# Shift rows as VectorE sums and late corrections in the first part of a hybrid-attention layer

## Chip, cores and metric

The kernel runs on one core of one Trainium2 chip. The metric is the device time of one execution in microseconds (us). The kernel before takes 2448.01 us, the median of three runs (2447.83 to 2448.09).

## The reference, cut to what matters

One transformer layer of width 2048 works on 512 latent tokens and 256 context tokens, in float32:

```python
mod_x = silu(c) @ w_ada + b_ada            # 6 x 2048 values for the latents
mod_c = silu(c_ctx) @ w_ada + b_ada        # the same for the context
h  = rmsnorm(x, norm1_w)   * (1 + s1)  + sh1     # shift sh1 and scale s1 from mod_x
hc = rmsnorm(ctx, norm1_w) * (1 + s1c) + sh1c    # from mod_c
p  = h @ w_in ;  pc = hc @ w_in            # queries, keys, values of 8 + 8 heads
x  = x + g1 * (attention heads of p, pc) @ w_o
x  = x + g2 * conv_ffn(modulate(rmsnorm(x, norm2_w), sh2, s2))
```

The change concerns sh1, s1 and the product with w_in. That product is linear: shifting the tokens by sh1 adds the vector sh1 @ w_in to every row of p.

## The kernel before

Tokens stand transposed: 16 tiles (kt) of 128 model channels, each with 512 latent columns and 256 context columns. Every float32 operand of a large product is cut into a rounded high half and the rest (ScalarE casts the high half, VectorE subtracts; `split`, lines L80 and L81), and `mm3` multiplies high by high, high by low and low by high (L104 to L106). Weight blocks are loaded raw (wr) and split into wh and wl, three buffers each. In the rows below a2k and c2k are token tiles, kh and kl split results on their way to DRAM, s and b accumulators in PSUM.

The stages up to the first head are:

- **First features.** The squares of the tokens are summed for the norm. Then for each unit of two kt the modulation is made: `scales` multiplies four 512 KB loads (adak) with silu(c) on TensorE (16 products, L219) and turns the result with `sel` (L223); `shifts` makes sh1 for both kt. For even kt it is four row sums of 1024 on VectorE (L251). For odd kt it is 16 transposes on TensorE (L258), four ScalarE copies (wt, L259) and 16 products (L219 with wt). Tokens get norm, scale and shift (L330 to L333) and go through `mm3` against five blocks of w_in: the four accumulators for latents and context, and one for the first query.
- **Features.** Seven blocks of 128 features (`feature`), each with rope, split and a write to DRAM (`keys`); then three blocks for the compressed query (`cq`) without context.
- **Values.** `for half in range(2)`: eight weight blocks each, 288 products, six accumulators; then each accumulator is split through two kvs buffers and written to v_d, from SP's queue for half 0 and from POOL's for half 1.
- **First head.** Its keys (ks, L527) are read back from DRAM; the score products are L482.

64 later values of the modulation are gemvs: `gemv` loads a row block of 1 MB (ada) over SP's queue into one of two buffers, and VectorE sums it (L171). 48 of them are handed out by `next_gemv` between the blocks of the features and values: 3 per feature, 2 per cq block, 1 or 2 per block of values. The order on each engine is set by a scheduler that follows the program's order where data and buffers allow; from the MLP on it is written by hand.

## Time and profile before

| | us |
|---|---|
| median of three runs | 2448.01 |
| profiled execution | 2454.1 |
| its span | 2451.9 |
| TensorE matmuls busy in the span | 2375.5 |
| VectorE busy | 1726.3 |
| ScalarE busy | 1102.5 |

The profiled execution is one run under the profiler, 2.2 us longer than its span; the mean granted TensorE clock was 0.988. The stretches named in the prediction are us from the span's start. Engines: PE is TensorE, DVE VectorE, ACT ScalarE, POOL GpSimd, SP SyncE, which issues most transfers. "L171" is line 171 of the kernel. In the lists of groups stand line, engine, operation, output and inputs, shapes and count, then busy time, mean ns of one, and idle time before it with what ended it.

### The profile page before, as it was taken

What the parts mean: (1) busy time and instruction counts of PE and PEld (TensorE: products, weight loads), DVE (VectorE), ACT (ScalarE), POOL (GpSimd) and SP (SyncE); (2) the same over time, 40 slices, a digit from 0 to 9 for tenths busy, and PEclk for the clock granted to TensorE, in tenths of its full rate; (3) what the DMA queues carried; (4) which work ended last, traced back from release to release, by engine and by line L of the source; (5) the groups of instructions that cost most, each with busy time, mean ns of one, the idle gap of its engine ahead of it and who ended that gap; (6) DMA issues with size and microseconds to landing.
All of it is one profiled execution on the core that took longest, in us unless ns stands there. A gap on an engine that the chain in (4) does not pass through costs nothing.

```text
span 2451.9 us, 32940 instructions
## 1 busy us (share of the span) xinstructions
PE 2375.5 (97%) x12788; PEld 1988.9 (81%) x12788; DVE 1726.3 (70%) x2272; ACT 1102.5 (45%) x1666; POOL 242.1 (10%) x270
## 2 busy tenths in 40 slices
PE   7999999999999999999999999999999999999997
PEld 3778887877777778888888888888888888888887
DVE  4668785388868877377666666666666666666667
ACT  4342121155545542244545454545454545454553
POOL 0000000122100003100111111111111111111113
PEclk8999999999999999999999999999999999999999
DMA  7868898554411149423555655555555555555572
GB/s 276 283 228 297 321 340 289 189 181 137 141 59 44 44 159 337 152 85 112 134 141 135 141 135 141 134 142 134 140 135 143 133 143 133 144 132 142 133 213 78
DMA packets 130706, 403.31 MB, mean 164 GB/s; under 512 B 14323, under 2 KB 25075, under 8 KB 122099
## 3 DMA queue, kind: packets, MB, share of 16 engines
q1 hardware_dynamic: 104118, 350.87, 43.4%
q0 software_dynamic: 25280, 49.30, 11.5%
q8 instruction: 100, 1.64, 0.3%
q10 hardware_dynamic: 1152, 1.05, 0.1%
q14 instruction: 56, 0.46, 0.1%
HBM read 331.68 MB, written 69.48 MB: 164 GB/s over the span
## 4 chain that ended last, share of the span: by engine, by line
PE 84%; DVE 8%; ACT 3%; DMA 3%; issue 1%; POOL 1%; SPq 0%; DVEq 0%; ACTq 0%; POOLq 0%
PE y L973 12%; PE b L105 10%; PE b L104 10%; PE b L106 10%; PE z L973 6%; PE y L975 6%; PE z L975 3%; PE s L104 3%; PE s L105 3%; PE s L106 3%; PE s L482 3%; PE x L973 2%; DMA ada<-in_ada 2%; PE x L975 1%; PE f L104 1%
## 5 line engine op out<-in xcount | busy, mean ns | idle before, releaser
L104 PE MATMUL b<-ah,wh 128*128 128x512 f32 (+1 forms) x672 | 259.1, 386 | 0.0
L105 PE MATMUL b<-al,wh 128*128 128x512 f32 (+1 forms) x672 | 259.0, 385 | 0.0
L106 PE MATMUL b<-ah,wl 128*128 128x512 f32 (+1 forms) x672 | 258.0, 384 | 0.0
L994 POOL DMA_DIRECT2D x_d<-xs x160 | 139.7, 1003 | 1166.4 <-ACT xs L993 1164.3
L949 DVE TENSOR_TENSOR wl<-wr,wh 128x1024 fp32r<-128x1024 f32 x126 | 153.8, 1221 | 128.7 <-ACT wh L943 128.7
L949 DVE TENSOR_TENSOR wl<-rb,wh 128x1024 fp32r<-128x1024 f32 x124 | 151.2, 1220 | 128.0 <-ACT wh L943 128.0
L80 ACT CAST wh<-wr 128x1024 fp32r<-128x1024 f32 (+3 forms) x118 | 115.9, 982 | 259.0 <-PE b L105 68.3
L943 ACT CAST wh<-wr 128x1024 fp32r<-128x1024 f32 x126 | 132.3, 1050 | 206.3 <-PE b L105 100.7
L943 ACT CAST wh<-rb 128x1024 fp32r<-128x1024 f32 x124 | 130.2, 1051 | 190.0 <-PE b L105 112.5
L949 DVE TENSOR_TENSOR wl<-ws,wh 128x1024 fp32r<-128x1024 f32 x123 | 150.1, 1221 | 88.8 <-ACT wh L943 88.8
L81 DVE TENSOR_TENSOR wl<-wr,wh 128x1024 fp32r<-128x1024 f32 (+3 forms) x118 | 137.3, 1164 | 89.4 <-ACT wh L80 89.0
L171 DVE CUSTOM_DVE_ANT_0 ada<-ada,cb,smt 128x2048 f32<-128x2048 f32 x64 | 151.6, 2369 | 62.4 <-DMA ada<-in_ada 62.1
L943 ACT CAST wh<-ws 128x1024 fp32r<-128x1024 f32 x123 | 128.3, 1043 | 137.0 <-PE b L105 45.2
L106 PEld LDWEIGHTS b<-ah,wl 128*128 128x128 f32 x672 | 126.3, 188 | 25.6
L104 PEld LDWEIGHTS b<-ah,wh 128*128 128x128 f32 x672 | 126.6, 188 | 22.9
L105 PEld LDWEIGHTS b<-al,wh 128*128 128x128 f32 x672 | 126.6, 188 | 22.0
L104 PE MATMUL b<-a2k,wh 128*128 128x512 f32 (+1 forms) x352 | 133.1, 380 | 6.6 <-ACT a2k L756 5.0
L106 PE MATMUL b<-a2k,wl 128*128 128x512 f32 (+1 forms) x352 | 132.5, 376 | 0.0
L973 PE MATMUL y<-b2k,wh 128*128 128x512 f32 x410 | 106.9, 390 | 0.0
L484 DVE TENSOR_REDUCE m<-s 128x1 f32<-128x768 f32 x96 | 90.5, 949 | 15.3 <-PE s L482 14.9
L993 ACT ACTIVATE xs<-b,modx 128x512 f32<-128x512 f32 x160 | 101.0, 680 | 0.5 <-PE y L973 0.3
L973 PEld LDWEIGHTS y<-b2k,wh 128*128 128x128 f32 x410 | 77.0, 188 | 17.1
(471 smaller groups left out, 5937.4 us busy)
## 6 DMA issues: line engine op xcount, KB each, us to landing
ada<-in_ada SPq DMA_DIRECT2D x64, 1024.0 KB, 6.8
rb<-in_w_up SPq DMA_DIRECT2D x123, 512.0 KB, 4.4
wr<-in_w_dn SPq DMA_DIRECT2D x84, 512.0 KB, 4.3
x_d<-xs POOLq DMA_DIRECT2D x160, 256.0 KB, 6.0
wr<-in_w_up SPq DMA_DIRECT2D x53, 512.0 KB, 4.2
wr<-in_w_f SPq DMA_DIRECT2D x34, 512.0 KB, 5.9
adak<-in_ada_k SPq DMA_DIRECT2D x32, 512.0 KB, 6.2
ada<-in_ada SPq DMA_DIRECT2D x32, 512.0 KB, 6.6
```

Of the source, the lines that this page charges most:

```text
L80: sc.copy(dst_h, src)
L81: ve.tensor_tensor(dst_l, src, dst_h.bitcast(F32), op=ALU.subtract)
L104: pe.matmul(out, st[0], mv[0], start=start, stop=False, **kw)
L105: pe.matmul(out, st[0], mv[1], start=False, stop=False, **kw)
L106: pe.matmul(out, st[1], mv[0], start=False, stop=stop, **kw)
L171: ve.tensor_tensor_reduce(out=junk, in0=w, in1=vec, op0=ALU.mult, op1=ALU.add, scale=1.0, scalar=col("b_ada", j), accum_out=dst[:, j:j + 1])
L943: sc.copy(hi, raw)
L949: ve.tensor_tensor(lo, raw, hi.bitcast(F32), op=ALU.subtract)
L973: pe.matmul(o, w[j][0], hs[j], start=start and j == 0, stop=False, skip_group_check=True)
L975: pe.matmul(o[:, h0], w[j][1], hs[j][:, h0], start=False, stop=j == 7, skip_group_check=True)
L993: sc.mul(x, po, modx[:, 80 + dt:81 + dt])
L994: gp.dma_start(x1_d[dt], x, accum_op=ALU.add)
```

## The change

The whole stretch from the start to the end of the first half of the values is written out in one order for all five engines; the code behind it is left to the scheduler.

- Scale products run one unit ahead, from eight loads of 256 KB per unit. Squares use the weight buffers.
- `shifts` is gone: no transposes, wt copies or wt products. A shift is now two row sums of 2048 on VectorE (`row_sum`), its 1 MB row loaded over POOL's queue (`row_load`).
- In the first features only kt 8 to 15 are shifted; kt 0 to 7 go in unshifted. The five results, and the sixth from an early feature that follows, are kept raw. During the early feature and the first half of the values VectorE sums the rows of kt 0 to 7, and `add_shift` adds them to the tokens, which are split again. The first half of the values takes the blocks in the order 4 to 7, 0 to 3.
- `bias_products` makes what the unshifted tokens lack in the six raw results, sh1 times w_in, in four steps, one behind each half of the next two features; it loads these weights again over POOL's queue, into the two ada buffers. `with_bias` adds it on ScalarE. The keys, first query and latent norm made from raw results move behind the second and third of these features.
- All gemv loads go over POOL's queue. Counts: 1 for each of the last three blocks of the first half of values, 2, 2, 2 and then 3 per feature, 3 per cq block and 3 per block of the second half. The second half's value writes stay on POOL.

```diff
-    def gemv(pool, j, srcs, bufs=2):
+    def gemv(pool, j, srcs, bufs=2, queue=None):
...
-        nc.sync.dma_start(w, ada[j])
+        (queue or nc.sync).dma_start(w, ada[j])
...
-        wt = st.tile([P, KT, P], F32, tag="wt", name=nm("wt"), bufs=1)
-        for q in range(4):
-            for i in range(4):
-                k = (q % 2) * 4 + i
-                pe.transpose(acc[:, i * P:(i + 1) * P], ws[q // 2][:, k * P:(k + 1) * P], ident)
-            sc.copy(wt[:, 4 * q:4 * q + 4].rearrange("p k f -> p (k f)"), acc)
-        products(lambda kt: wt[:, kt], P)
-        for i, d in enumerate(dst):
-            ve.tensor_scalar(out=d, in0=acc[:, i:i + 1], scalar1=col("b_ada", kt), scalar2=None, op0=ALU.add)
...
+    KA, EARLY = 8, 1
+    KB = ((4, 5, 6, 7, 0, 1, 2, 3), tuple(range(8)))
...
+    def row_load(kt):
+        rows[kt] = sp_.tile([P, D], F32, tag="ada", name=nm("ada"), bufs=2)
+        gp.dma_start(rows[kt], ada[kt])
+
+    def row_sum(kt, i):
+        w = rows[kt]
+        vec, m = ((cb, modx), (ccb, modc))[i]
+        out = w if i else sp_.tile([P, D], BF16, tag="junk", name=nm("junk"), bufs=1)
+        ve.tensor_tensor_reduce(out=out, in0=w, in1=vec, op0=ALU.mult, op1=ALU.add, scale=1.0,
+                                scalar=col("b_ada", kt), accum_out=m[:, kt:kt + 1])
+
+    def add_shift(kt, tmp):
+
+        for i, (hl, m, n_) in enumerate(((hx[kt], modx, T), (hc[kt], modc, C))):
+            t = tmp()[:, :n_]
+            ve.tensor_tensor(t, hl[0].bitcast(F32), hl[1].bitcast(F32), op=ALU.add)
+            split_hl(hl, t, m[:, kt:kt + 1])
...
+        def scale_load(u):
+            wks[u] = []
...
+            for j in range(8):
+                wk = st.tile([P, 2, 2 * P], F32, tag="adak", name=nm("adak"), bufs=9)
+                nc.sync.dma_start(wk, ada_k[u, j // 4][:, (j % 4) * 2:(j % 4) * 2 + 2])
+                wks[u].append(wk)
...
+        def tokens_b(kt):
+            h = hs.pop(kt)
+            for hl, c, m in ((hx[kt], slice(0, T), modx), (hc[kt], slice(T, TT), modc)):
+                split_hl(hl, h[:, c], m[:, kt:kt + 1] if kt >= KA else None)
...
+        due = [(kt, i) for kt in range(KA, KT) for i in range(2)][1:]
+        NU = KT // 2
+        for u in range(NU):
+            if u + 2 < NU:
+                scale_load(u + 2)
+            raws_ = [wraw(w_g0[kt], 640) for kt in (2 * u + 2, 2 * u + 3)] if u + 1 < NU else []
+            if u + 2 < NU:
+                row = scale_products(u + 2)
+            if u + 1 < NU:
+                for kt in (2 * u + 2, 2 * u + 3):
+                    tokens_a(kt)
+                for kt, raw in zip((2 * u + 2, 2 * u + 3), raws_):
+                    if kt >= KA:
+                        while due and due[0][0] <= kt:
+                            row_sum(*due.pop(0))
+                    tokens_b(kt)
+                    block_g0(raw)
+            else:
+                ahead(2)
+            first_features(2 * u)
+            if u + 2 < NU:
+                scale_turn(u + 2, row)
+            for _ in range(2 if u else 3):
+                if due:
+                    kt, i = due.pop(0)
+                    row_sum(kt, i)
+                    if i and kt + 2 < KT:
+                        row_load(kt + 2)
+            first_features(2 * u + 1)
...
-                gemv(pool, j, [(cb, modx)])
-
-    lo, hi = slice(0, 64), slice(64, 128)
+                gemv(pool, j, [(cb, modx)], queue=gp)
...
-    latent_norm(ckv, TT, KVR, "kvn", ckv_d)
-    for f in range(7):
-        lat, co = b_tile(), s_tile()
-        feature(lat, co[:, :C])
-        keys(k_d[f + 2] if f < 6 else kr_d, lat, co[:, :C])
-        next_gemv(kv, 3)
-    cq = []
-    for i in range(3):
-        lat = b_tile()
-        feature(lat, None)
-        t = kv.tile([P, TT], F32, tag="lt", name=nm("cq"), bufs=3)[:, :T]
-        sc.copy(t, lat)
-        cq.append(t)
-        next_gemv(kv, 2)
...
-            next_gemv(kv, 1 if (half * 8 + kb) % 3 else 2)
...
+        raws[4] = keep(lat0[4], None, rawq)
+        for f in (2, 3, 0, 1):
+            raws[f] = keep(lat0[f], ctx0[f])
+        todo = [(kt, i) for kt in range(KA) for i in range(2)]
+
+        def sums_of_rows(count):
+            for _ in range(count):
+                if todo:
+                    kt, i = todo.pop(0)
+                    row_sum(kt, i)
+                    if i and kt + 2 < KA:
+                        row_load(kt + 2)
+
+        def early(hf):
+            sums_of_rows(2)
+            ahead(2)
+
+        elat, eco = b_tile(), s_tile()
+        feature(elat, eco[:, :C], early)
+        raws[5] = keep(elat, eco[:, :C])
+
+        def upper(n_):
+            ahead(2)
+            if n_ < 4:
+                sums_of_rows(3)
+                for kt in ((0, 1), (2,), (3,), (4, 5))[n_]:
+                    add_shift(kt, rtmp)
+            elif n_ == 4:
+                for kt in (6, 7):
+                    add_shift(kt, rtmp)
+            else:
+                next_gemv(sp_, 1)
+
+        vo0 = values(0, upper)
...
+        w = sp_.tile([P, D], F32, tag="ada", name=nm("bw"), bufs=2)
+        if step < 3:
+            kts = range(3 * step, min(3 * step + 3, KA))
+            for i, kt in enumerate(kts):
+                gp.dma_start(w[:, i * 640:(i + 1) * 640], w_g0[kt])
+            for i, kt in enumerate(kts):
+                r = slice(32 * (kt % 4), 32 * (kt % 4) + 32)
+                o = i * 640
+                pe.matmul(ac[0][r], spad[:, kt], w[:, o:o + 512], start=kt < 4, stop=kt >= KA - 4)
+                pe.matmul(ac[1][r, :P], spad[:, kt], w[:, o + 512:o + 640], start=kt < 4, stop=kt >= KA - 4,
+                          skip_group_check=True)
+            return
+        gp.dma_start(w[:, :1024], w_f[0, 0])
+        for kt in range(KA):
+            r = slice(32 * (kt % 4), 32 * (kt % 4) + 32)
+            pe.matmul(ac[1][r, P:2 * P], spad[:, kt], w[:, kt * P:(kt + 1) * P], start=False, stop=kt >= KA - 4,
+                      skip_group_check=True)
+        for n_, c in enumerate((4, 2)):
+            row = rtmp()
+            sc.copy(row[:, :c * P], ac[n_][:, :c * P])
+            for i in range(c):
+                pe.matmul(ac[n_][:, 2 * i:2 * i + 2], row[:, i * P:(i + 1) * P], sel, start=True, stop=True)
+            ve.tensor_copy(beta[:, 8 * n_:8 * n_ + 2 * c], ac[n_][:, :2 * c])
...
+    for f in range(EARLY, 7):
+        lat, co = b_tile(), s_tile()
+        n_ = 2 * (f - EARLY)
+        feature(lat, co[:, :C], (lambda hf: bias_products(n_ + hf)) if n_ < 4 else None)
+        keys(k_d[f + 2] if f < 6 else kr_d, lat, co[:, :C])
+        if n_ == 2:
+            for i in range(2):
+                t = with_bias(2 + i)
+                keys(k_d[i], t[:, :T], t[:, T:])
+            q = rtmp()
+            apply_rope(q, with_bias(4), rtmp)
+            put(q0_d, stacked_queries(kvs, q, DA_SCALE))
+        elif n_ == 4:
+            t = with_bias(5)
+            keys(k_d[2], t[:, :T], t[:, T:])
+            latent_norm([with_bias(i) for i in range(2)], TT, KVR, "kvn", ckv_d)
+        next_gemv(sp_, 2 if n_ < 6 else 3)
+    cq = []
+    for i in range(3):
+        lat = b_tile()
+        feature(lat, None)
+        cq.append(keep(lat, None)[:, :T])
+        next_gemv(sp_, 3)
+    latent_norm(cq, T, QR, "qn", cq_d)
+    vo1 = values(1, lambda n_: next_gemv(sp_, 3))
+    put_values(1, vo1)
```

How the rows move is shown at three places. `order` rows hold line, operation, output and inputs, shape, and the number of equal rows in a run.

**PE in the first features.** Before, the odd kt's transposes (ident, ada), products (wt) and the turn (sel) stand between the feature products:

```order
L104 MATMUL s_428<-a2k_1390,wh_1160 128x512
L258 MATMUL b_189<-ident,ada_1166 128x128 x4
L105 MATMUL s_428<-a2k_1391,wh_1160 128x512
L106 MATMUL s_428<-a2k_1390,wl_1161 128x512
L104 MATMUL b_187<-c2k_1388,wh_1160 128x256
L104 MATMUL s_428<-a2k_1390,wh_1160 128x512
L219 MATMUL b_189<-wt_1168,cpad 32x128 x16
L105 MATMUL b_187<-c2k_1389,wh_1160 128x256
L106 MATMUL b_187<-c2k_1388,wl_1161 128x256
L105 MATMUL s_428<-a2k_1391,wh_1160 128x512
L223 MATMUL b_189<-sel,row_1205 128x2
```

Now only the scale products of a unit ahead stand there, eight rows in one run ahead of the unit's features, of which the last are shown (the turn of the unit before stands between the features of its two kt):

```order
L316 MATMUL b_338<-adak_605,cpad 32x256 x2
L316 MATMUL b_338<-adak_607,cpad 32x256 x2
L316 MATMUL b_338<-adak_609,cpad 32x256 x2
L316 MATMUL b_338<-adak_611,cpad 32x256 x2
L107 MATMUL b_335<-a2k_505,wh_519 128x512
L108 MATMUL b_335<-a2k_506,wh_519 128x512
L109 MATMUL b_335<-a2k_505,wl_520 128x512
```

The rows with ident and wt are gone from this stage.

**VectorE among the features.** Before, one feature's gemvs (ada) and one key's rope (rt, kl) stand between two splits of weights (wl):

```order
L723 SCALAR_TENSOR_TENSOR a_93<-modx,smt 128x1
L171 ISA ada_2471,modx<-ada_2471,cb_1730,smt 128x2048
L171 ISA modx 128x1
L149 TENSOR_TENSOR rt_2454<-b_2344,ropet 128x512
L150 STREAM_SHUFFLE rt_2455<-b_2344 128x512
L81 TENSOR_TENSOR kl_2461<-s_2345,kh_2460 128x256
L151 TENSOR_TENSOR rt_2455<-rt_2455,ropet 128x512
L171 ISA ada_2474,modx<-ada_2474,cb_1730,smt 128x2048
L171 ISA modx 128x1
L152 TENSOR_TENSOR rt_2454<-rt_2454,rt_2455 128x512
L81 TENSOR_TENSOR wl_2578<-wr_2575,wh_2577 128x1024
```

Now, ahead of the second split of the fifth feature (wl_2685; the first is 57 rows before, with ten gemvs, five ropes and the latent norm, nr, between), the last rows are:

```order
L174 ISA ada_2974,modx<-ada_2974,cb,smt 128x2048
L174 ISA modx 128x1
L164 TENSOR_SCALAR rt_2542<-s_2532 128x512
L165 SCALAR_TENSOR_TENSOR rt_2543<-nr_2541 128x512
L166 TENSOR_TENSOR rt_2543<-rt_2543,rt_2542 128x512
L174 ISA ada_3040,modx<-ada_3040,cb,smt 128x2048
L174 ISA modx 128x1
L167 SCALAR_TENSOR_TENSOR nr_2541<-rt_2543,nr_2541 128x512
L164 TENSOR_SCALAR rt_2550<-s_2532 128x256
L165 SCALAR_TENSOR_TENSOR rt_2551<-nr_2541 128x256
L81 TENSOR_TENSOR wl_2685<-wr_2682,wh_2684 128x1024
```

Work of earlier features, the raw results' ropes and gemvs of later ones now stand in one piece ahead of this split.

**VectorE and SP at the end of the second half of values.** Before, no gemv stands there; the splits of the value results (kl) follow those of the weights:

```order
L81 TENSOR_TENSOR wl_3670<-wr_3667,wh_3669 128x1024
L81 TENSOR_TENSOR wl_3715<-wr_3712,wh_3714 128x1024
L81 TENSOR_TENSOR wl_3760<-wr_3757,wh_3759 128x1024
L81 TENSOR_TENSOR wl_3766<-wr_3763,wh_3765 128x1024
L81 TENSOR_TENSOR kl_3770<-s_3399,kh_3769 128x512
L81 TENSOR_TENSOR kl_3776<-s_3399,kh_3775 128x512
L81 TENSOR_TENSOR wl_4052<-wr_4049,wh_4051 128x1024
L81 TENSOR_TENSOR kl_3782<-s_3400,kh_3781 128x512
L81 TENSOR_TENSOR kl_3788<-s_3400,kh_3787 128x512
```

Now the last gemvs stand ahead of them:

```order
L81 TENSOR_TENSOR wl_3633<-wr_3630,wh_3632 128x1024
L174 ISA ada_3576,modx<-ada_3576,cb,smt 128x2048
L174 ISA modx 128x1
L174 ISA ada_3579,modx<-ada_3579,cb,smt 128x2048
L174 ISA modx 128x1
L81 TENSOR_TENSOR kl_3637<-b_3235,kh_3636 128x512
L81 TENSOR_TENSOR kl_3643<-s_3233,kh_3642 128x512
L81 TENSOR_TENSOR wl_3925<-wr_3922,wh_3924 128x1024
L81 TENSOR_TENSOR kl_3649<-s_3233,kh_3648 128x512
L81 TENSOR_TENSOR kl_3655<-s_3234,kh_3654 128x512
L81 TENSOR_TENSOR kl_3661<-s_3234,kh_3660 128x512
```

On SP, with waits shown, the first keys before:

```order
L90 DMA wr_4303<-in_w_f 128x1024 [waits DMAHW6_49,DMAHW1_49,DVE_49]
L515 DMA qs_3821<-q_d 128x512
L515 DMA qs_3822<-q_d 128x512 [waits DMAHW3_49]
L527 DMA ks_3825<-k_d_128 64x2x768 [waits PE_49]
L528 DMA klz_3815<-k_d_128 64x768
```

and now:

```order
L680 DMA qs_3694<-q_d 128x512 [waits PE_49,Pool_49]
L680 DMA qs_3695<-q_d 128x512 [waits DMASW2_49,DMASW6_49,DVE_49,PE_49]
L692 DMA ks_3698<-k_d_128 64x2x768 [waits DMASW5_49,DMASW3_49,DMASW7_49,DMASW1_49,DVE_49]
L693 DMA klz_3688<-k_d_128 64x768
L692 DMA ks_3698<-k_d_128 64x2x768
```

The first load of ks waited for PE alone; now it waits for transfers of POOL's queue (DMASW, the value writes) and DVE.

More of the change, by code (lines that the diff above doesn't have):

```diff
@@ L415, in latent_norm, with keep, feature @@
             put(dst[i], hl)
-    ckv = []
-    for i in range(2):
-        t = kv.tile([P, TT], F32, tag="lt", name=nm("ckv"), bufs=3)
-        sc.copy(t[:, :T], lat0[i])
-        sc.copy(t[:, T:], ctx0[i])
-        ckv.append(t)
-    keys(k_d[0], lat0[2], ctx0[2])
-    keys(k_d[1], lat0[3], ctx0[3])
-    q = rtmp()
-    apply_rope(q, lat0[4], rtmp)
-    put(q0_d, stacked_queries(kv, q, DA_SCALE, 1))
-    def feature(lat, ctxo):
+    def keep(lat, co, t=None):
+        t = t or raw_tile("raw")
+        sc.copy(t[:, :T], lat)
+        if co is not None:
+            sc.copy(t[:, T:], co)
+        return t
+    def feature(lat, ctxo, between=None):
         for hf in range(2):
@@ L464, in layer_kernel, with put_values @@
                     src, o = (hx[kt], t * P) if t < 4 else (hc[kt], (t - 4) * P)
[L465 to L466 removed]
+                    mm3(vo[t], (src[0][:, o:o + P], src[1][:, o:o + P]), w, n_ == 0 and j == 0, n_ == 7 and j == 1)
+            between(n_)
         ahead(2)
+        return vo
+    def put_values(half, vo):
         for t in range(NKEY):
@@ L1194, in layer_kernel @@
     bp.release()
+    wrp.release()
 def _rope_tables(np):
```

343 lines of the change are left out of this document (192 added, 151 removed).

## The prediction

> **What bounds the kernel now.** I read the busy time by stretches first (us, then busy time and records of PE, PEld, DVE, ACT and POOL, granted clock, DMA share, GB/s):
>
> ```profile
> span 2451.9 us, 32940 instructions
> ...
> 60.00:182.00 122.00, 119.73 (x1019) 92.16 (x1019) 81.39 (x156) 45.69 (x88) 0.00 (x0) 1.00 0.75 257
> 200.00:345.00 145.00, 145.00 (x774) 123.62 (x772) 117.91 (x147) 32.96 (x43) 0.00 (x0) 1.00 0.88 327
> 345.00:415.00 70.00, 65.42 (x289) 53.66 (x287) 49.69 (x50) 11.44 (x14) 0.00 (x0) 0.99 0.84 301
> 500.00:2452.00 1952.00, 1907.59 (x10153) 1621.10 (x10152) 1398.72 (x1810) 956.92 (x1435) 228.81 (x247) 0.99 0.49 135
> ```
>
> TensorE (PE) bounds every stretch. Its instructions behind 500 us keep their order (only 16 row loads change queue there), so the end moves by what the first head's score products move. Six points on the chain of waits (start us, us, what) date the way there:
>
> ```profile
> 52.37 1.22 PE s L104 x2
> ...
> 77.51 1.01 PE b L219 x32
> ...
> 93.67 1.01 PE b L219 x32
> ...
> 182.72 0.72 DVE rt L150
> ...
> 414.98 0.76 PE s L104
> ...
> 486.16 9.22 DMA klz<-k_d
> ```
>
> The old order: first features from 52.4, one unit (two token tiles) per 16.1 us (93.67 - 77.51), done near 182.7; second half of the values from 415.0, done some 65 us later; score products from about 495 (486.16 + 9.22, the first keys landing). Between 182 and 500 us PE waits over 2 us only twice, 9.5 us in all (waits of PE: us, times, longest):
>
> ```profile
> PE s L482 <- DMA ks<-k_d: 4.9, 1, 4.9
> PE s L104 <- DVE kl L81: 4.6, 1, 4.6
> ```
>
> **Term 1, first features: -31 us.** The groups of the window 60 to 182, which holds seven units (count, busy us, mean ns of one, idle before), on PE and then on VectorE (DVE):
>
> ```profile
> L258 PE MATMUL b<-ident,ada 128*128 128x128 f32 x112 | 17.7, 280 | 1.4 <-ACT wt L259 1.4
> L219 PE MATMUL b<-adak,cpad 128*32 128x256 f32 x224 | 14.4, 384 | 0.0
> L219 PE MATMUL b<-wt,cpad 128*32 128x128 f32 x224 | 7.6, 276 | 0.0
> ```
>
> ```profile
> L81 DVE TENSOR_TENSOR wl<-wr,wh 128x640 fp32r<-128x640 f32 x14 | 11.5, 820 | 0.1
> L333 DVE SCALAR_TENSOR_TENSOR a2k<-h,modx,a2k 128x512 fp32r<-128x512 f32 x15 | 11.2, 750 | 5.8 <-ACT a2k L332 5.8
> ...
> L333 DVE SCALAR_TENSOR_TENSOR c2k<-h,modc,c2k 128x256 fp32r<-128x256 f32 x15 | 7.2, 479 | 0.0
> ```
>
> Removed per unit: 17.7/7 + 7.6/7 = 3.6 us of PE, so a unit is 12.5 us. The scale products stay (14.4/7 = 2.1), one unit ahead, so the last two units lack them. The start slips: the first tokens now want the scales of two units ahead of them in PE's queue, and the third unit's loads follow the first's products; I take 56, between 52.4 (no slip) and 60 (one more load of 7 us); the other edits ahead of it (squares in the weight buffers, the norm in halves) lie inside this number. The stage ends at 56 + 8 x 12.5 - 2 x 2.1 = 152 instead of 182.7. Cover: DVE per unit has two row sums of 2048 (2 x 2.35, the gemv's row below), four token operations of 0.75 and four of 0.48, two splits of 0.82: 11.3 us. That fits under 12.5, with nothing to spare; without that cover each excess us counts eight times. DMA is no worse: 257 GB/s at a share of 0.75, and half the shift rows move later.
>
> **Term 2, early feature and first values: +9 us over PE's own work.** A product of 512 columns costs 65.42/289 = 0.226 us of PE, one half of the values (288) 65.4, a feature without context (48) 10.9. A whole feature takes 16.8, as ScalarE's casts of successive context halves show (start us, us):
>
> ```profile
> 239.05 0.37 ACT L80 CAST kh<-s 128x256 fp32r<-128x256 f32 x1 [7.42 <-PE s L106]
> ...
> 255.85 0.37 ACT L80 CAST kh<-s 128x256 fp32r<-128x256 f32 x1 [4.42 <-PE s L106]
> ```
>
> With 2 us for the copies the values start at 152 + 2 + 16.8 = 171. The groups of DVE between 182 and 500, and of ScalarE between 60 and 182:
>
> ```profile
> L171 DVE CUSTOM_DVE_ANT_0 ada<-ada,cb,smt 128x2048 f32<-128x2048 f32 x48 | 112.8, 2349 | 50.5 <-DMA ada<-in_ada 50.2
> L81 DVE TENSOR_TENSOR wl<-wr,wh 128x1024 fp32r<-128x1024 f32 x40 | 48.8, 1221 | 28.1 <-ACT wh L80 27.9
> L152 DVE TENSOR_TENSOR rt<-rt,rt 128x512 f32<-128x512 f32 x10 | 6.9, 685 | 0.0
> ```
>
> ```profile
> L332 ACT ACTIVATE a2k<-h,modx 128x512 fp32r<-128x512 f32 x14 | 10.1, 724 | 5.8 <-DVE modx L262 5.1 <-DVE modx L251 0.7
> ```
>
> Between two weight splits stand three row sums (7.05), the split (1.22) and one or two added shifts. A shift is 0.69 + 0.75 on DVE for the latents, an estimated 0.4 + 0.48 for the context, and two ScalarE turns that it waits for (0.72, and an estimated 0.5): 3.5. So DVE takes 12 to 15 us where PE takes 8.2. Three split buffers and the blocks that need no shift absorb most; the sixth block's split comes about 7 us late, two smaller waits add 2. Values end at 171 + 65.4 + 9 = 245.
>
> **Term 3, features and correction: +33 us over PE's own work.** Six features and three without context are 6 x 16.8 + 3 x 11 = 134 us; before, the same ran without a wait (145.00 of 145). The four steps add 4 us of PE: 8 products of 512 columns at twice a scale product (2.1/16 = 0.13), 16 of 128 at 7.6/7/16 = 0.07, and the turns. Each step reads weights through the two row buffers, loaded only when released, so PE or the next gemv waits; the bounds are 0 and four loads of 7, I take 5, since most of a load runs under the half before it. The large piece is a stall. Between the two weight splits of the fifth feature DVE's order holds 10 gemvs (24.3 with 0.08 each for reading the sum), five rope turns of four operations (0.69, the shuffle a little more), their splits, the raw query and the latent norm: 47.4 us. The first of the two splits reuses the buffer that the third feature's last product frees. From there PE has three halves of latent products (24 x 0.226 = 5.4 each), the norm's sums (an estimated 2) and the fourth feature's context half (16.8 - 10.9 = 5.9): 24 us. So PE stands 47.4 + 1.2 - 24 = 24 us, however early DVE was; behind it wait the evacuation of keys and so the score tiles. The second values start at 245 + 134 + 4 + 5 + 24 = 412 (before: 415).
>
> **Term 4, second values and first head: +27 us against the old order.** Now 17 of the 48 gemvs remain, two ahead of each split. Their pace, one load of 1 MB per freed buffer, from the chain between 364 and 374 us, and the landing times (KB each, median us) of other loads between 400 and 500:
>
> ```profile
> 364.13 7.53 DMA ada<-in_ada
> 371.68 2.35 DVE ada L171
> 374.07 7.40 DMA ada<-in_ada
> ```
>
> ```profile
> v_d<-kh SPq DMA_DIRECT2D x6, 256.0 KB, 6.7
> v_d<-kl SPq DMA_DIRECT2D x6, 256.0 KB, 6.2
> v_d<-kh POOLq DMA_DIRECT2D x6, 256.0 KB, 5.6
> v_d<-kl POOLq DMA_DIRECT2D x6, 256.0 KB, 7.0
> ```
>
> Two buffers and a turn of 7.4 + 2.35 give 4.9 us each; DVE alone would take 2.43 (2.35 and the read). The loads now go over POOL's queue, on which the value writes of one size land as soon as on SP's (6.3 against 6.5 in the mean). I take 4.5, near the measured end, with a little off since the old gemvs ran at a DMA share of 0.84: 17 x 4.5 = 77. What queues behind the last gemv is the value evacuation, six splits with two buffers, each waiting for writes of 6 to 7 us: 17, a last write 6, then the keys' load, 7 (9.2 in the row of the chain, among more transfers): 30. The keys' load newly waits for these writes; before it waited for PE alone, and ran beside them. Score products at 412 + 77 + 30 = 519, against 495: +24. The rest is the same (of the 16 rows that change queue late, none is near PE: its idle there is 1952 - 1907.6 = 44 us in all), so the profiled execution of 2454.1 us (span 2451.9 and 2.2 around it) becomes 2478. The runs' median is 2448.0, 6 us below that execution, so I predict 2472.
>
> The Trainium skill, "SBUF — State Buffer", section "SBUF: two separate sides", speaks against the moved loads: descriptors of a transfer issued from GpSimd wait while VectorE holds the shared port pair. By it each gemv load could start up to one gemv (2.35 us) later, and the sum would be up to 17 x 2.35/2 = 20 us more. The write rows above show no such delay, though for smaller transfers and an idler VectorE.
>
> **Rivals.** (a) PE paces all of it: DVE reaches the fifth feature's second split in time because loads over POOL's queue arrive earlier, or PE has more in hand than I count. Then the second values start at 171 + 65.4 + 134 + 4 = 374, and with the gemvs at DVE's own pace scores come 65.4 + 30 later, at 470: 25 us ahead, 2423; with half of the 38 us of waits left, 489, 2442. Time 2430. For it: DVE was busy 118 us of 145 in the feature stretch and PE never waited. Against: the same DVE work plus 16 row sums and eight shifts now stands behind a shorter PE.
> (b) The gain is just used up: the stall at the fifth feature is a third (8) and the gemvs take 4.2: 2472 - 16 - 5 = 2451. Nothing in the profile favours just this sum.
> (c) Loads over POOL's queue each wait for the VectorE operation running: the first stage's eight rows come late too (8 x 1.2 = 10) and term 4 grows by 20. 2472 + 30 = 2502, slower still.
> (d) That the first stage does not shorten, because its row loads set the unit, I give no chance of its own: 8 rows of 1 MB at 7.4 us are 59 us even one by one, under its 100.
>
> **Numbers.** What one can tell from no change is 0.2%, 4.9 us. My forecast 0.48, its own range 2459 to 2493: at the low end the gemvs keep up with PE's 65.4 (412 + 65.4 + 30 = 507), at the high end they take 4.9 (+7), with 4 us more in term 2 and 10 in term 3. (a) 0.30; (b) 0.14, mostly within 0.2%; (c) 0.08. Faster 0.30, same 0.12, slower 0.58. The range 2426 to 2495 leaves out the better third of (a) and most of (c).
>
> **What would show it.** Right: the last first-feature product near 152; a PE wait of 7 us on a weight split in the first values; one of some 20 us, on a VectorE result, in the fourth or fifth feature; gemvs 4 to 5 us apart until after the second values; the keys' load issued about 20 us after PE's last value product. Wrong in term 1: unit over 13 us. Wrong in term 3: no PE wait over 10 us between 245 and 412. Wrong in term 4: last gemv done before the last value product. If PE shows no waits at all, (a) holds and the time is near 2425 to 2430.

## The result, and the profile after

The changed kernel takes 2488.7 us (median of four runs, 2482.7 to 2497.5) against 2448.05 us of the kernel before: 1.0166 times as long, with a 95% interval of 1.0134 to 1.0199, or 40.6 us more. The forecast was 2472, in a range of 2426 to 2495. The profiled execution of the changed kernel took 2491.0 us, its span is 2489.2 us.

The first view is again busy time by stretches (us, then busy time and records of PE, PEld, DVE, ACT and POOL, granted clock, DMA share, GB/s). The stretches are cut at the changed kernel's own steps: first features, first values, the features with the correction, the stretch with the stall, second values, and the way to the first scores; the rest of the features, 345 to 422, is left out.

```profile
span 2489.2 us, 32361 instructions
...
60.00:152.00 92.00, 91.61 (x619) 75.62 (x618) 79.74 (x112) 28.98 (x54) 4.75 (x9) 1.00 0.77 265
166.00:242.00 76.00, 67.80 (x287) 54.78 (x286) 61.11 (x72) 19.18 (x28) 5.61 (x11) 0.96 0.42 147
242.00:300.00 58.00, 54.70 (x322) 45.41 (x321) 30.31 (x44) 15.45 (x25) 6.91 (x13) 0.94 0.81 283
300.00:345.00 45.00, 23.50 (x106) 18.74 (x105) 40.01 (x65) 8.39 (x15) 4.22 (x8) 0.80 0.89 304
...
422.00:498.00 76.00, 69.13 (x293) 55.48 (x291) 55.51 (x54) 14.42 (x18) 9.63 (x18) 0.98 0.86 314
498.00:533.00 35.00, 12.55 (x45) 9.88 (x45) 11.02 (x12) 3.83 (x6) 11.30 (x16) 0.66 0.65 207
```

Before, PE was busy in 145.00 of the 145 us between 200 and 345. Now it is full in the first features, and has smaller gaps in both halves of the values and holes of 21.5 us (300 to 345) and 22.5 us (498 to 533). Where it stands idle the granted clock falls as well: 0.80 and 0.66. The waits of PE between 130 and 540 us (us, times, longest) name the holes:

```profile
PE s L470 <- ACT nq L468: 26.9, 3, 21.5
PE f L107 <- DVE kl L81: 23.0, 1, 23.0
PE b L107 <- ACT wh L80: 7.0, 2, 6.2
PE s L107 <- DVE rt L164: 5.4, 1, 5.4
```

L470 is the latent norm's sum of squares, L468 the squares on ScalarE that it sums (nq), `f` the accumulator of the first head's feature, L80 the cast ahead of a split, L164 an operation of the norm's root on VectorE. What ScalarE did just ahead of these squares (start us, us, what, and in brackets the idle time before it with what ended it):

```profile
341.80 0.62 ACT L80 CAST kh<-rt 128x512 fp32r<-128x512 f32 x1 [8.53 <-DVE rt L155]
342.32 0.84 ACT L468 ACTIVATE nq<-raw 128x768 f32<-128x768 f32 x1
349.69 0.84 ACT L468 ACTIVATE nq<-raw 128x768 f32<-128x768 f32 x1 [6.53 <-DMA k_d<-kh]
```

So the first and longer wait is one on VectorE's backlog: in ScalarE's order the squares stand behind the cast of a key, and that cast waits for a rope on VectorE (rt, L155). The second squares wait for the write of a key out of their buffer. These points of the timeline date the steps (same columns):

```profile
67.45 1.93 PE L316 MATMUL b<-adak,cpad 128*32 128x256 f32 x32
79.74 1.93 PE L316 MATMUL b<-adak,cpad 128*32 128x256 f32 x32
...
148.19 0.59 ACT L482 COPY raw<-s 128x512 f32<-128x512 f32 x1 [0.95 <-PE s L109]
...
223.24 0.80 PE L107 MATMUL b<-wh,a2k 128*128 128x512 f32 x1 [6.21 <-ACT wh L80]
242.10 0.39 PE L109 MATMUL b<-wh,c2k 128*128 128x512 f32 x1
249.42 0.55 PE L107 MATMUL s<-c2k,wh 128*128 128x256 f32 x1 [3.30 <-DVE a L888]
343.21 2.93 PE L470 MATMUL s<-nq,ones 128*128 128x512 f32 x4 [21.50 <-ACT nq L468]
350.59 2.93 PE L470 MATMUL s<-nq,ones 128*128 128x512 f32 x4 [4.45 <-ACT nq L468]
422.31 0.79 PE L107 MATMUL b<-wh,a2k 128*128 128x512 f32 x1
506.94 2.35 DVE L174 CUSTOM_DVE_ANT_0 ada<-ada,cb,smt 128x2048 f32<-128x2048 f32 x1 [3.05 <-DMA ada<-in_ada]
519.66 0.69 DVE L81 TENSOR_TENSOR kl<-b,kh 128x512 fp32r<-128x512 f32 x1
520.41 0.79 PE L107 MATMUL f<-a2k,wh 128*128 128x512 f32 x1 [22.95 <-DVE kl L81]
533.18 0.47 PE L647 MATMUL s<-ks,qs 128*128 128x512 f32 x1 [0.22 <-DMA ks<-k_d]
```

A unit of the first features takes 12.3 us (79.74 - 67.45), and these features are copied out at 148.2. The last product of the first values starts at 242.1, so they end near 242.4. The second values start at 422.3 and end at 520.41 - 22.95 = 497.5. The last gemv ends at 509.3, the last clearing of a value tile at 520.35, and the first score products start at 533.2, where the kernel before has them at 495. That is 38 us later. Behind them the two spans are nearly equal: 2489.2 - 533.2 = 1956 us, against 2451.9 - 495.2 = 1956.7.

### The profile page after: what moved, and what is told of

It reads as the page before. It is cut to its first block, busy times and chain, and to the rows that moved or that the text cites. A ratio compares the mean times of both kernels' runs of the same rounds, so it can differ in the third digit from the quotient of the medians.

```text
span 2489.2 us, 32361 instructions
## 1 busy us (share of the span) xinstructions
PE 2362.3 (95%) x12448; PEld 1976.4 (79%) x12448; DVE 1772.0 (71%) x2300; ACT 1099.7 (44%) x1666; POOL 284.8 (11%) x362
## 3 DMA queue, kind: packets, MB, share of 16 engines
q10 hardware_dynamic: 1152, 1.05, 0.1%
## 4 chain that ended last, share of the span: by engine, by line
PE 66%; issue 18%; DVE 9%; ACT 3%; POOL 2%; DMA 2%; SPq 0%; POOLq 0%; DVEq 0%; ACTq 0%
PE y L1138 12%; PE b L107 8%; PE b L108 8%; PE b L109 8%; PE z L1138 6%; PE y L1140 6%; PE z L1140 3%; PE x L1138 2%; PE s L107 2%; PE s L109 2%; PE s L108 1%; PE x L1140 1%; POOL ada L171 1%; DVE p L705 1%; DVE m L649 1%
## 5 line engine op out<-in xcount | busy, mean ns | idle before, releaser
L80 ACT CAST wh<-wr 128x1024 fp32r<-128x1024 f32 (+3 forms) x118 | 115.5, 980 | 265.2 <-PE s L108 92.2
L1114 DVE TENSOR_TENSOR wl<-ws,wh 128x1024 fp32r<-128x1024 f32 x123 | 150.1, 1220 | 88.7 <-ACT wh L1108 88.7
```

What stands on the lines that cost most here:

```text
L80: sc.copy(dst_h, src)
L1114: ve.tensor_tensor(lo, raw, hi.bitcast(F32), op=ALU.subtract)
```

## The experiments

Two things had to be told apart first: how much of the time the gemvs cost at all, and whether single long waits set the end or the amount of work that VectorE has before the first head.

### No gemvs before the first head

```
             j = next(gv, None)
-            if j is not None:
+            if j is not None and j >= 80:
```

> The changed kernel without the 48 gemvs of the features and values (their loads and sums are left out, the modulation values they make are zeros). Theory (VectorE's order holds up PE): 24 of the 47 us of VectorE work between the two splits of the fifth feature are gone, so the PE wait of 21.5 + 4.5 us there falls under 6 us, the lower clock behind it goes too, and the value results are cleared right behind the last value product instead of 12 us later: 2489 - 26 - 5 - 12 = about 2446, at most 2455. Rival (the correction and PE's own order hold it up, not the gemvs): the wait at the norm's sums stays, only the 12 us at the end go: about 2477.

Measured: 2437.5 us (2431.3 to 2439.3), ratio 0.9954 [0.9940, 0.9969]. The theory was right in direction, and its time somewhat too high. The longest wait of PE, same stretch and columns as above:

```profile
PE f L107 <- DVE kl L81: 10.2, 1, 10.2
```

Both waits at the norm are gone (0.5 us remain); 10.2 us before the first head's feature are left, on the clearing of the values, which six splits with two buffers take even without a gemv ahead of them. So the 48 gemvs cost the changed kernel 2488.7 - 2437.5 = 51 us. The kernel leaves out their loads and their sums at once, so it can't tell the two apart; in the second values of the changed kernel VectorE spends more on the sums (44.6 us) than on waiting for their loads (27.8). Without them the new order beats the old one, which has its 48 gemvs, by 11 us in the medians; the old order without gemvs was not run. In the traces the first scores stand 23.8 us ahead of the old kernel's (471.4 against 495.2), and about 7 us of this go in the projection: from the last transpose of the attention weights on PE to the projection's last residual on VectorE it takes 176.8 us, against 169.7 before.

### The latent norm two features later

```
-        elif n_ == 4:
+        elif n_ == 10:
             t = with_bias(5)
```

> The changed kernel with one move: the third key from the early feature and the latent norm stand behind the seventh feature instead of the fourth. Theory (PE stands in its own order at the norm's sums, waiting through ScalarE for VectorE's backlog): with the norm two features later the backlog runs beside PE's products and the 21.5 us wait shrinks to under 8: 2489 - 20 = about 2466 (2458 to 2474). Rival (VectorE's total work binds, the wait only changes place): PE waits as much elsewhere, 2482 to 2492.

Measured: 2484.4 us (2477.9 to 2498.3), 1.0158 [1.0124, 1.0192]: the rival. The waits of PE in this kernel, same stretch and columns as above:

```profile
PE f L107 <- DVE kl L81: 36.9, 1, 36.9
PE s L470 <- ACT nq L468: 9.8, 2, 7.7
```

The norm's waits fall from 26.9 to 9.8 us, and the one before the first head grows from 23.0 to 36.9. The wait was moved, not removed: what VectorE has to do before it clears the last values is the same, and PE waits for it in one place or the other. All its waits in this stretch add up to 67.9 us in the changed kernel and to 63.9 here.

### Fewer gemvs before the first head

Fourteen of the 48 go to the output projection, behind the attention, where now every weight block takes one row.

```
-    gv = iter([64 + i ...] + [48 + i for i in range(16)] + [32 + i ...])
+    gv = iter([64 + i ...] + [32 + i ...] + [48, 49])
...
-    gv = iter([80 + i for i in range(16)])
+    gv = iter([50 + i for i in range(14)] + [80 + i for i in range(16)])
```

> The changed kernel with 14 of the 48 gemvs moved to the output projection, where free places are left. Theory (the last gemvs stand ahead of the clearing of the value results): no gemv is left when the last value product is done, the clearing starts 11 us earlier, and the first score products with it: 2489 - 11 = 2478 (2473 to 2482), with no loss in the output projection. Rival (the clearing is late anyway, or the projection pays for it): 2485 to 2495.

Measured: 2498.3 us (2491.8 to 2501.2), 1.0204 [1.0188, 1.0219]: slower even than the rival. The wait before the first head falls to 10.5 us, as wanted, but the gain is lost in the projection. Its waits (930 to 1110 us), first in the changed kernel, then in this one:

```profile
PE b L109 <- DVE wl L81: 2.6, 1, 2.6
PE s L109 <- DVE wl L81: 1.4, 1, 1.4
```

```profile
PE b L109 <- DVE wl L81: 10.2, 3, 6.1
PE s L109 <- DVE wl L81: 4.7, 2, 3.8
```

The projection has no room for 30 gemvs either: from the last transpose of the attention weights to the last residual it takes 190.2 us, against 175.7 in the changed kernel. The norm's waits are 3.7 us longer too (30.6 against 26.9).

### All row loads on SyncE's queue

```
-                gemv(pool, j, [(cb, modx)], queue=gp)
+                gemv(pool, j, [(cb, modx)])
```

> The changed kernel with the loads of all 64 gemvs back on SP's queue. Theory (the queue of the loads does not matter, VectorE's order does): within 6 us of the changed kernel, 2483 to 2495; gemvs 4 to 5 us apart as before. Rival (loads from POOL's queue come late because they wait for the VectorE operation running): faster by 10 to 20, 2470 to 2479, with gemvs nearer to each other.

Measured: 2460.8 us (2451.6 to 2466.6), 1.0051 [1.0028, 1.0074]. Both theories missed: 28 us of the 40 are gone. The waits of PE up to the first head:

```profile
PE f L107 <- DVE kl L81: 17.0, 1, 17.0
PE s L470 <- ACT nq L468: 14.8, 1, 14.8
```

Against the changed kernel's waits the norm takes 12.1 us less, the wait on the root (5.4) is gone, the one before the first head is 6.0 shorter, and so is the projection (169.7 against 175.7, measured as above): 29.5 in all, where the two profiled spans differ by 30.0 and the medians by 28. In the stretch of the stall the loads themselves are not what got faster. Landing times of the row loads (KB each, median us from issue), between 300 and 400, 400 and 440, and 440 and 520 us, in the changed kernel:

```profile
ada<-in_ada POOLq DMA_DIRECT2D x16, 1024.0 KB, 6.9
ada<-in_ada POOLq DMA_DIRECT2D x9, 1024.0 KB, 5.6
ada<-in_ada POOLq DMA_DIRECT2D x13, 1024.0 KB, 6.9
```

And with all of them on SyncE's queue:

```profile
ada<-in_ada SPq DMA_DIRECT2D x16, 1024.0 KB, 7.1
ada<-in_ada SPq DMA_DIRECT2D x10, 1024.0 KB, 5.1
ada<-in_ada SPq DMA_DIRECT2D x13, 1024.0 KB, 5.4
```

What differs is VectorE's order, which in this part of the program is left to the scheduler. The gemvs between the two weight splits of the fifth feature, in the changed kernel and then in this one (count, busy us, mean ns, idle before them):

```profile
L174 DVE CUSTOM_DVE_ANT_0 ada<-ada,cb,smt 128x2048 f32<-128x2048 f32 x10 | 23.5, 2347 | 6.5 <-DMA ada<-in_ada 6.5
```

```profile
L174 DVE CUSTOM_DVE_ANT_0 ada<-ada,cb,smt 128x2048 f32<-128x2048 f32 x7 | 16.4, 2349 | 4.0 <-DMA ada<-in_ada 4.0
```

Three gemvs with their share of waiting for loads are 7.1 + 2.5 = 9.6 of the 12.1 us. At the end of the second values the last gemvs stand between the splits that clear the values, where the changed kernel has all of them ahead of the clearing. That this order is the cause, and not the queue as such, was not tried alone; that the loads land no sooner in the stretch of the stall is what the rows show.

### Only the sixteen late rows on SyncE's queue

```
-                gemv(pool, j, [(cb, modx)], queue=gp)
+                gemv(pool, j, [(cb, modx)], queue=gp if pool is sp_ else None)
```

> The changed kernel with only the 16 gemv loads of the output projection back on SP's queue; the 48 early ones stay on POOL's. Theory (their queue costs the projection 4.5 us, the rest of what SP's queue gained lies in the early order): 2489 - 4 = 2484 (2480 to 2488). Rival (POOL's queue costs most of the 28 us in the projection and behind it): under 2470.

Measured: 2487.8 us (2479.0 to 2490.6), 1.0149 [1.0125, 1.0173]. The rival is out. In the trace PE's two waits on weight splits in the projection (4.0 us) are gone, and the projection, measured as above, is back from 175.7 to 169.7 us, the length it had before. That is 6.0 us; the 4.5 of the expectation counted from a wait of VectorE in one kernel and from its first residual in the other. The stretch behind the projection is 3.3 us longer in this execution (1392.4 against 1389.1), for a reason that was not traced. The median moved by 1 us only, within the scatter, so the 6 us are read from the trace and not from the times.

### Both at once, then the clearing as well

Rows on SyncE's queue and the late norm together:

> Loads of the gemvs on SP's queue and the latent norm behind the seventh feature. Theory (two waits on VectorE's order that add: the backlog ahead of the fifth feature's split, and gemvs among the clearing of the last values): the 14.8 us wait at the norm's sums goes and about as much is gained, 2461 - 13 = 2448 (2442 to 2454). Rival (VectorE's total work binds, so the wait moves to the end as it did with POOL's queue): 2456 to 2464.

Measured: 2458.4 us (2445.0 to 2464.4), 1.0030 [1.0013, 1.0047]: the rival. The norm's wait is down to 4.0 us, and 21.0 remain before the first head. So the next kernel also puts the clearing of the second values ahead of other work on VectorE, and clears the two tiles first that the next products want:

```
-    put_values(1, vo1)
+    with tc.high_priority():
+        put_values(1, vo1)
...
-        for t in range(NKEY):
+        for t in (0, 5, 1, 2, 3, 4) if half else range(NKEY):
```

It also gives the first head's tiles memory of their own, so that the keys' loads needn't wait for the clearing.

> As the kernel with SP's queue and the late norm, and besides the clearing of the last values is given priority, starts with the two accumulators that the next feature needs, and the first head's keys go to memory that no value result holds. Theory (the head's start waits for the clearing): some 8 us earlier, about 2441 (2434 to 2447). Rival (gemvs still stand among the clearing and set its pace): no gain over that kernel, 2446 to 2454.

Measured: 2452.2 us (2439.1 to 2456.5), 0.9995 [0.9975, 1.0014], at the rival. In the profiled execution, the fastest of the ten and 13 us under their median, the wait before the first head is 3.5 us, but VectorE's splits of that feature's weights now come late (6.5 us); the 12.6 us of waits on casts of weights are no news, the kernel just above had 13.3. With seven gemvs moved on to the projection:

> As the kernel before in this call, and 7 of the 48 early gemvs moved to the output projection, so that none is left when the last value product is done. Theory: the clearing runs alone, first score products some 10 us ahead of the old kernel's, 2434 (2427 to 2441), below the kernel before the change. Rival (the projection pays for its seven, as it paid 13 us for fourteen): 2441 to 2450.

Measured: 2446.9 us (2435.9 to 2456.7), 0.9991 [0.9973, 1.0010]. The rival again: no wait of that stretch is over 6.3 us in the profiled execution, and the median is still only level with the kernel before the change. That execution took 2435.9 us, the fastest of ten and 11 us under the median, so its profile doesn't show what the median pays for.

### Is term 2 a cost of its own, and is the stall set by what stands between two splits?

The next kernel leaves the work out whose price term 2 gave.

```
-        todo = [(kt, i) for kt in range(KA) for i in range(2)]
+        todo = []
...
-                for kt in ((0, 1), (2,), (3,), (4, 5))[n_]:
-                    add_shift(kt, rtmp)
```

> The changed kernel without the sixteen row sums of the first eight tokens, their loads and the eight added shifts (these shifts are zero): 67 us less work on VectorE before and in the first values. Theory (term 2 as predicted, and the stall at the fifth feature is fixed by what stands between its two weight splits, however early VectorE is): the 6.2 us wait in the first values goes, the wait of some 24 us at the fifth feature stays, 2480 (2476 to 2484). Rival (VectorE's backlog builds up from the first values on, so the stall shrinks as well): stall under 10 us and 2455 to 2468.

Measured: 2480.8 us (2475.0 to 2489.4), 1.0137 [1.0115, 1.0160]: the theory. The longest waits of PE:

```profile
PE s L468 <- ACT nq L466: 30.7, 3, 23.3
```

The 6.2 us in the first values are gone, and the time falls by 8. The stall is as long as before (23.3 against 21.5 in its first part), though VectorE has some 53 us less to do (busy 1718.7 against 1772.0 us in all; the 67 of the expectation holds the turns on ScalarE too). In that stretch an earlier VectorE is no help: the cast ahead of the fifth feature's first split waits 3.47 us for PE to free its buffer in both kernels, as the prediction had it, and what counts is the work that stands behind that split.

### The start

Ten profiles showed the first scale products anywhere between 30.4 and 41.5 us (the last section). The next two kernels take products out of that stretch: VectorE adds twelve of the sixteen squared tokens, not eight.

```
-            if kt % 2 == 0 and kt:
+            if kt % 4 != 1 and kt:
                 ve.tensor_tensor(sqs, sqs, sq[:, :TT], op=ALU.add)
```

> The changed kernel, with four of the sixteen squared tokens summed by TensorE instead of eight; VectorE adds the other twelve. Theory (the start is paced by TensorE, whose products take twice as long for the first 14 to 30 us, a time that differs between executions; first scale products at 30.4 to 41.5 us in the ten profiles so far): four groups of 1.5 to 2.9 us go, the first scale products stand at 30 to 35 us in any execution, the median falls from 2488.7 to 2483 (2479 to 2486) and the runs lie closer together. Rival (the start does not set the end, or the slow stretch only moves to later products): 2486 to 2491, same scatter.

Measured: 2492.3 us (2488.8 to 2494.7), 1.0181 [1.0167, 1.0195]. The median didn't fall, so the rival holds there; the runs lie within 6 us instead of 15, but these are four runs each.

> The version with all mends (rows on SyncE's queue, norm late, clearing first, seven row sums moved to the output projection: 2446.9) and the squares summed as in the run beside it. Theory (TensorE's slow start costs up to 11 us, 5 in the mean): 2442 (2437 to 2445), below the kernel before by 0.2 to 0.4 percent. Rival: 2446 to 2448, no difference to the kernel before.

Measured: 2446.1 us (2439.2 to 2450.2), 0.9986 [0.9977, 0.9995]: 2 us below the kernel before, which is under the 0.2% that count as a difference. The mend didn't hold its bound of 35 us, since the last sum now waits for VectorE (4.2 us in the one profile, 2.9 in the other) and its products then run slowly again: 2.8 to 2.9 us for four where 1.45 is the usual time. In the first of the two kernels the slow stretch ended as early as in the fastest profiles (13.7 us), and the first scale products still came at 34.3 us, not at 30.4 or 30.5 as there. In the second they stand at 38.1. None of the kernels that do the whole computation beats the old order by more than that.

## Why the prediction was right or wrong

The direction and the range were right, and so was the cause of the loss, VectorE's work between the points where PE needs it. The place of the first stall was wrong, some terms were mis-sized, and the time was 16.7 us too low. Point by point:

**Term 1 held.** 152 was forecast for the end of the first features and 148.2 came; the unit is 12.3 us, not 12.5, so rival (d), that this stage does not shorten, is out.

**Term 2 held.** The wait on the sixth block's split is 6.2 us against "about 7", the values end at 242.4 against 245, and leaving the late shifts out gave 8 us against 9. The end hides two small misses: the values start at 165.8, not 171, and take 76.6 us, not 74.4.

**Term 3 was too small by 13 us; this is the first step that failed.** From the end of the first values to the start of the second, 167 us were forecast (412 - 245) and 180 came (422.3 - 242.4). The forecast had 138 of PE's own work and 29 of waits. The same stretch, which holds the same products, in the changed kernel and then in the kernel without gemvs:

```profile
242.40:422.30 179.90, 150.12 (x793) 124.34 (x792) 129.31 (x177) 45.03 (x68) 17.98 (x34) 0.91 0.85 297
```

```profile
236.50:381.10 144.60, 144.04 (x792) 120.47 (x791) 69.53 (x107) 45.95 (x69) 1.60 (x3) 1.00 0.46 159
```

The sum of the waits came out, 179.9 - 150.1 = 29.8 us, but partly by luck. The correction's steps cost no wait, where I took 5, and 3.3 us that I had not looked for stand at the first feature behind the values, on a small operation of VectorE by the profile. The stall is 21.50 + 4.45 = 26 against 24, but in another place. The forecast let PE run the norm's sums and the fourth feature's context half and then stand at the fifth feature's second split. In the trace PE stops at the norm's sums, since their squares wait in ScalarE's order for a rope that is itself part of VectorE's backlog. From the freed buffer (the cast at 305.3) PE had 16.4 us in hand there, the three latent halves alone, and not 24; the rope it waited for was done at 341.8, some 35 us behind the first split, while the second split came at 359.8 and cost PE no wait. So the forecast had both sides of its difference too large (48.6 and 24 for 37.9 and 16.4 us, up to the first sum at 343.2), and the wait for a key's write, 4.45, makes up the rest.

What was mis-sized in the sum is PE's work, in two parts. Its products at full speed take 144 us, not 138. The correction's products are a part of this: 4.4 us in the two largest groups between 246 and 292 us, and 1.1 in two smaller ones, against 4 (count, busy us, mean ns, idle):

```profile
L583 PE MATMUL b<-bw,rt 128*32 128x512 f32 x16 | 3.2, 605 | 0.0
L584 PE MATMUL b<-bw,rt 128*32 128x128 f32 x16 | 1.2, 273 | 0.0
```

Another is the latent norm's sums, the other 4 us or so, which I had used as cover for the stall and not added to the work. The second part is the speed: with the waits, the mean granted clock of the stretch is 0.91 instead of 1.00, and the same products take 150.1 - 144.0 = 6.1 us longer. The forecast charged each wait at its length and each product behind it at full speed.

**Term 4 had the right pace, too few gemvs and a wrong last step.** From the second values' start to the scores 107 us were forecast (77 + 30), and 110.9 came. The gemvs between 423 and 509 us:

```profile
L174 DVE CUSTOM_DVE_ANT_0 ada<-ada,cb,smt 128x2048 f32<-128x2048 f32 x19 | 44.6, 2351 | 27.8 <-DMA ada<-in_ada 27.8
```

Nineteen in 86.1 us are 4.5 each, the pace taken, but two more than the 17 that I counted. The last one ends 11.8 us after the last value product. The second latent norm adds a wait of 5.4 us inside the second values, where VectorE is late with its root; it is no loss by itself, since the gemvs set this end. Clearing takes 11 us. But what the clearing holds up is not the keys' load, for which the scores wait 0.2 us; it is the accumulator of the first head's own feature, for which PE waits 23 us, and the half of that feature that has to run before the scores (520.4 to 533.2). The keys load beside it. From the last gemv to the scores this makes 24 us instead of 30.

**Rows that change queue late** were said to cost nothing. In the trace the projection is 6.0 us longer: PE waits 2.6 + 1.4 on weight splits in it, and no longer does with these rows on SyncE's queue. I had read PE's small idle time there as a sign that nothing was near it; it meant that there was no slack either.

**The sum** in the profiled execution: the scores start 14.2 us later than forecast (-2.6 up to the end of the first values, +13 in term 3, +3.9 in term 4). Behind them the span is 0.7 us shorter than before, although it holds the 6.0 us of the late rows: the stretch up to the last transpose of the attention weights took 391.2 us against 393.5, and the one behind the projection 1389.1 against 1393.5, which I did not trace further (it lies between 1390.9 and 1393.4 in the profiles of the experiments). The old scores stood at 495.2 and not 495, and 0.4 us less lie outside the span. So 2491.0 came against 2478. The last 4 us are chance, the step from one execution to the median: it was 6 us above the median before, and is 2 above it now.

**Rivals.** (a), that PE sets the pace, was wrong: the kernel comes near it (2437.5 against 2430) only without the gemvs. (b), the gain just used up by a stall of 8 us and gemvs 4.2 apart, did not come: they are 26 and 4.5. That the order with every mend is level with the old one (2446 to 2452) is another kernel's sum. (c), loads that wait for VectorE's running operation, is not supported. The Trainium skill, "SBUF — State Buffer", section "SBUF: two separate sides", has a transfer issued from GpSimd wait for its descriptors while certain operations of VectorE hold the port pair that the two share; if the row sums are among them, each load could start up to one of them late. The rows above show 6.9, 5.6 and 6.9 us on POOL's queue against 7.1, 5.1 and 5.4 on SyncE's, so no delay in the stretch of the stall, and at most 1.5 us in the last. That 1.5 does not follow the queue: in the same window the median is 6.5 us on SyncE's queue with the late norm, and 5.5 on POOL's in the kernel that has only the late rows on SyncE's. The queue did matter, by more than (c) gave it (28 us), but beside it stands another order of VectorE, which was not tried alone, and not later landings.

## What to carry to other kernels

When a short stage sheds work onto an engine that is not the bottleneck, count that engine's whole backlog up to the next point where the bottleneck needs it: moving one stall from there only lengthens the next one (of 27 us at the norm 17 went, and the 23 at the first head became 37). Charge each wait of TensorE with the slow products behind it as well; here 30 us of waits made the same products 6 us slower. And the queue of a load is also an input to the scheduler: the same instructions with another queue came out in another order, with 28 us between the two.

## What the runs showed of the hardware

TensorE's slow stretch at the start ends at very different times. The same instructions (spread of the condition, L272, and sums of squares, L290) in the changed kernel:

```profile
6.99 3.78 PE L272 MATMUL b<-cb,ones 1*128 1x512 f32 x4 [6.99 <-ACT cb L276]
10.70 2.93 PE L290 MATMUL s<-sq,ones 128*128 128x512 f32 x4
...
26.69 3.78 PE L272 MATMUL b<-ccb,ones 1*128 1x512 f32 x4
...
39.78 1.93 PE L316 MATMUL b<-adak,cpad 128*32 128x256 f32 x32
```

And in the kernel with rows on SyncE's queue, late norm and early clearing:

```profile
7.15 3.78 PE L272 MATMUL b<-cb,ones 1*128 1x512 f32 x4 [7.15 <-ACT cb L276]
10.86 2.93 PE L290 MATMUL s<-sq,ones 128*128 128x512 f32 x4
13.71 2.11 PE L272 MATMUL b<-cb,ones 1*128 1x512 f32 x4
15.75 1.56 PE L290 MATMUL s<-sq,ones 128*128 128x512 f32 x4
...
30.48 1.93 PE L316 MATMUL b<-adak,cpad 128*32 128x256 f32 x32
```

Four products take 3.78 and 2.93 us while PE is slow, and 2.11 and 1.56 after it, and PE works without a gap in both. The load on the DMA engines is not what differs: between 12 and 30 us their busy share is 1.05 in both. In one execution the slow stretch ends at 13.7 us, in the other past 30, and the first scale products stand 9.3 us apart. The Trainium skill, "TensorE: Matmul & The Clock Gate", section "Part 1: The HAM clock gate (the "warmup" mystery)", gives about 3.4 us of sustained work before the clock rises and warns that the count of slow products varies from run to run; behind the wait at 520 us that fits here (the slow products end some 4 us later), at the start it doesn't: 6.6 us in the one, over 23 in the other. The granted-clock column of the profile shows 1.00 in that stretch, so only the durations tell.

This may be much of the scatter of the new order's runs. How far the profiled execution lay from its kernel's median goes with where its first scale products stood:

| first scale products, us | profiled execution minus median, us |
|---|---|
| 30.4 and 30.5 (two of the kernels with clearing first) | -11.0, -13.1 |
| 33.6, 33.6, 34.3 (no gemvs; late norm; sums on VectorE) | -6.2, +3.4, -3.5 |
| 36.8 and 38.1 (fewer gemvs; all mends and sums) | +0.1, +0.8 |
| 39.8 to 41.5 (the changed kernel and four others) | +2.3, +1.1, +4.8, +2.2, +0.2 |

It is a relation among twelve executions and no proof: the late norm's execution stands against it (33.6 us and +3.4), and the largest difference, 13.1 us, is more than the 11 between the earliest and the latest start. Why the slow stretch ends when it does stays open. The attempt to shorten it by the sums on VectorE didn't lower the changed kernel's median.
